# A late step of an attention block's end: moved by one or two tiles, in two parts, behind a product on GpSimd

## The chip, the cores and the metric

The kernel runs on one core of a Trainium2 chip. Its engines are TensorE (PE; its weight loads are shown as PEld), VectorE (DVE), ScalarE (ACT), GpSimd (POOL) and SyncE (SP, which here only issues DMAs). The metric is the device time of one execution in microseconds. Before the change it is 3525.12 us, the median of three runs that took 3520.41, 3525.12 and 3527.70 us. A separate profiled execution took 3519.81 us.

## The reference

A two-layer backbone over 2048 latent tokens (a grid of 32 rows by 64 columns, width 1024) with 256 context tokens. Layer 0 mixes latent attention and a gated linear attention; layer 1, which the change touches, is a two-dimensional neighbourhood attention with 16 heads of 64. What it computes, cut to this layer:

```python
# for each grid row r: kb, vb are the 8 rows of keys and values around r
s_lat = einsum('bqhd,brkhd->bhqrk', qr, kb) * scale + bias          # a table by row and column offset
s_lat = where(col_mask, s_lat, -inf)                                 # 16 columns around the query
s_ctx = einsum('bqhd,bchd->bhqc', qr, k_ctx) * scale                 # all 256 context keys
p = softmax(concatenate([s_lat, s_ctx], -1))
o = einsum('bhqk,bkhd->bqhd', p_lat, vb) + einsum('bhqc,bchd->bqhd', p_ctx, v_ctx)
# then
y = dot(o.reshape(..., 1024) * silu(z_x), w_out)
x = x + gate * y
```

Inputs and output are float32. Each query's output is a weighted sum of values, divided by the sum of its weights (the softmax's denominator), and then multiplied by the gate path's value.

## The kernel before

The whole program is written out by hand in Python and handed to a planner, which fixes the order of instructions on each engine: it simulates the engines and, whenever one is free, issues the ready instruction that was written first. `issue_after(ins)` adds an edge: what is written in its block and runs on the same engine as `ins` comes behind `ins`. Each engine then works through its own queue in the planned order.

The layer-1 attention (`odd_attention`) takes the 16 heads as 8 head pairs, j = 0 to 7; one head of a pair lies in partitions 0 to 63, the other in 64 to 127. The 2048 queries are four blocks of 512 (8 grid rows each), b0 to b3. The keys are 16 latent tiles of 128 keys (l0 to l15) and, for each block of queries, two context tiles of 128 keys. The list `units` gives a pair's 24 tiles in order: c0 twice, l0, c1 twice, l1 to l3, c2 twice, l4 to l7, c3 twice, l8 to l15.

For each tile PE makes scores (L1785, keys against the queries that can see them) into one of two PSUM tiles "st". For a latent tile, DVE adds the table of biases (L1963, "table sums", several instructions where the rectangle falls into pieces) into one of eleven SBUF tiles "opt", and ACT takes the exponential in place. For a context tile ACT takes it straight from PSUM. The products with the values come some tiles later: the list `pend` holds finished tiles, and whenever it holds five, at each second tile, `flush(2)` works off two. `tail_ctx` (L1797) makes a context tile's product with the values; the first of a block starts a new PSUM bank "o", of which there are four (L1794). `tail` (L1815) adds a latent tile's products to the banks of the blocks that it touches, and GpSimd adds the weights themselves to the running sums "oacc" (L1821), the later denominators. The first sums of a block are made from its two context tiles (L1806), on DVE for b0 and b2, on GpSimd for b1 and b3.

When the last latent tile of a block is done, `finish_blocks` ends the block. It is a generator, and each `yield` ends a step: (1) PE sums the denominators over the partitions, times -2 (L1838), into an "st" tile, ACT copies them; (2) ACT takes the logarithm (into "rl", of which there is one); (3) ACT takes the exponential of its negative, about the reciprocal; (4) a product of the two (L1849), on GpSimd for b0 and b3 of the pairs j = 0 to 6, else on DVE; (5) three DVE steps on the block's bank: a Newton step with that product (L1853), times the reciprocal (L1854), times the gate path's value "Z" (L1855); then a DMA of the result (L1856), on GpSimd's queue but for b0 of the last pair.

b0's generator is started and run to its end within one `flush` (L1915 to L1917). The others are appended to the list `ends`, and `end()`, called once a tile (L1972), takes one step of the first generator in the list, with edges behind this tile's exponential on ACT and behind the latest table sums on DVE. b1's end begins in the last tiles of its own pair, those of b2 and b3 in the next pair, after tiles l2 and l4. In the last pair b2 and b3 end together. The tiles of the gate path ("os4" and "ogate", loaded by `gates` on SP's queue, each with one buffer) are free again when L1855 has read them. In the last pair DVE and ACT also split the output weights between the tiles (L1299).

Of the kernel before, what the change touches and what calls it, by code (L numbers as in the profile page):

```python
# [88 lines left out]
class Kern:  # L89
# [1630 lines left out]
    def odd_attention(self, out, pools, left, wout):  # L1720

        nc = self.nc
        self.RT1 = self.scr("RT1", (KD, P, SEQ), F32)
        NR, NC = (len(b) for b in BLOCKS["k"])
        with ExitStack() as es:
# [62 lines left out]
            def sums(acc, bb, n=1):  # L1788

                return [acc[bb // 2][:, i].rearrange("p r c -> p (r c)")[:, (bb % 2) * 512 : (bb % 2) * 512 + n * 512] for i in range(2)]  # L1790
# [41 lines left out]
            def finish_blocks(bbs, j, O, acc):  # L1832

                n, hf, o0 = len(bbs), bbs[0] // 2, bbs[0] % 2 * 512
                den = both()
                for b, bb in enumerate(bbs):
                    for i, a in enumerate(sums(acc, bb)):
                        mm = nc.tensor.matmul(den[i * 64 : i * 64 + 64, b, :], self.mtwos[:], a, start=True, stop=True)  # L1838
                dc = exps()
                self.act(dc[:, :n], den[:, :n])  # L1840
                yield mm
                ln = self.tl(lp, [P, 2, 512], "rl", bufs=1)
                self.act(ln[:, :n], dc[:, :n], AF.Ln, scale=-1.0)
                yield
                rc = exps()
                self.act(rc[:, :n], ln[:, :n], AF.Exp, scale=-1.0)
                yield
                near = nc.gpsimd if bbs in ([0], [3]) and j < 7 else nc.vector
                near.tensor_tensor(out=ln[:, :n], in0=dc[:, :n], in1=rc[:, :n], op=ALU.mult)  # L1849
                yield  # L1850
                for b, bb in enumerate(bbs):
                    o = O.pop(bb)[:].rearrange("p r c -> p (r c)")
                    nc.vector.scalar_tensor_tensor(out=o, in0=ln[:, b], scalar=2.0, in1=o, op0=ALU.add, op1=ALU.mult)  # L1853
                    nc.vector.tensor_tensor(out=o, in0=o, in1=rc[:, b], op=ALU.mult)  # L1854
                    nc.vector.tensor_tensor(out=rc[:, b], in0=o, in1=Z[j, hf][:, o0 + b * 512 : o0 + b * 512 + 512], op=ALU.mult)  # L1855
                (nc.sync if (j, bbs) == (7, [0]) else nc.gpsimd).dma_start(self.RT1[j, :, bbs[0] * 512 : (bbs[0] + n) * 512], rc[:, :n].rearrange("p b c -> p (b c)"))  # L1856

# [45 lines left out]
            def flush(n):  # L1903

                mm = None
                for f, *a in pend[:n]:
                    mm = f(*a)
                del pend[:n]
                for x in late:
                    x[0] -= 1  # L1910
                for x in [x for x in late if x[0] <= 0]:
                    late.remove(x)
                    ends.append(finish_blocks(*x[1:]))
                    mm = next(ends[-1])
                    if x[1] == [0]:  # L1915
                        for _ in ends.pop():
                            pass  # L1917
                return mm
# [9 lines left out]
            for j in range(8):  # L1928
                OA[j] = {}, {}
                for s, (kind, n, u) in enumerate(units):  # L1930
                    g, c = divmod(n, 4)
# [183 lines left out]
            for t in range(PLAIN, NT - NCT, 2):  # L2115
# [3 lines left out]
                else:  # L2119
                    res = exps([P, 512])  # L2120
# [105 lines left out]
```

## Time and profile before

| What | Value |
|---|---|
| median of three runs | 3525.12 us (3520.41 to 3527.70) |
| the profiled execution | 3519.81 us, span from the first to the last instruction 3518.0 us |
| busy share of the span | PE 98%, DVE 68%, ACT 42%, GpSimd 30% |
| TensorE clock granted | 0.992 on average |
| layer-1 attention | about 2940 to 3370 us of the span; one head pair takes 46.5 us |

A row of a timeline gives the start in us from the span's start, the duration in us (of the whole run where a row stands for several of the same), the engine ("q" behind it is its instruction queue), the line, the operation, out<-in with the program's names, the shapes and the count; in brackets the idle time of the engine just before it, and which engine, tile and line ended it. A row of the waits reads: who waited, for whom, us in total, times, the longest. A row of stretches gives the stretch, its length, then busy us and instructions of PE, PEld, DVE, ACT and POOL, the granted clock, the share of the DMA engines and GB/s. "om,ones" marks the last of a tile's four score terms; 128x512 in L1785 is a context tile.

### The profile page before, as it was taken

Reading aid. Unit: us, or ns where it says so; the run is one execution under the profiler, and the core shown is the slowest. Engines: PE = TensorE matmul, PEld = TensorE weight load, DVE = VectorE, ACT = ScalarE, POOL = GpSimd, SP = SyncE. Lnnn points to the kernel's source line nnn. Section 1 sums busy time; section 2 is a strip of 40 time slices with the busy share of each in tenths; the row PEclk is TensorE's granted clock in tenths of the full one; section 3 lists DMA queues with packets and bytes.
Section 4 is the critical chain, followed back from the end, with each engine's and each line's share of the span. In section 5 each row is a group of like instructions: output and inputs, shape, how many; then the busy total and the mean of one; then the engine's idle time right before and its main releaser. Section 6 shows DMA issues by size and latency. Waiting matters only on the chain.

```text
span 3518.0 us, 54816 instructions
## 1 busy us (share of the span) xinstructions
PE 3431.9 (98%) x20228; PEld 2656.4 (76%) x20228; DVE 2405.5 (68%) x4509; ACT 1466.8 (42%) x2612; POOL 1061.2 (30%) x1309
## 2 busy tenths in 40 slices
PE   8999998999999999999999999999999999999899
PEld 6898987888886666665556888888888887555577
DVE  4677755888886777768877555555577884565765
ACT  4545552111113555456664345444422223555532
POOL 1343331111111334322211133333211113778711
PEclk9999999999999999999999999999999999999999
DMA  7555555232325242333634674444845546555374
GB/s 255 144 160 160 149 142 155 96 108 89 93 81 171 60 135 80 98 115 123 185 96 133 128 184 150 143 147 144 277 151 167 157 149 216 193 202 187 110 184 63
DMA packets 350111, 508.40 MB, mean 145 GB/s; under 512 B 32666, under 2 KB 233066, under 8 KB 342884
## 3 DMA queue, kind: packets, MB, share of 16 engines
q1 hardware_dynamic: 297364, 386.91, 36.3%
q0 software_dynamic: 29456, 82.14, 8.8%
q10 hardware_dynamic: 23024, 35.85, 3.0%
q8 instruction: 160, 2.62, 0.3%
q14 instruction: 107, 0.88, 0.1%
HBM read 325.99 MB, written 196.60 MB: 149 GB/s over the span
## 4 chain that ended last, share of the span: by engine, by line
PE 78%; DVE 6%; POOL 5%; DMA 5%; ACT 3%; issue 2%; SPq 1%; DVEq 0%; ACTq 0%; POOLq 0%
PE gm L133 10%; PE gm L131 10%; PE gm L132 10%; PE st L1175 10%; PE av L1085 7%; PE mx L705 4%; PE st L1785 2%; PE pu L1364 2%; PE o L1364 2%; POOL oacc L1821 2%; PE st L1364 1%; PE pj L1364 1%; PE mx L1697 1%; PE o L1815 1%; DMA adaw<-ada_w 1%
## 5 line engine op out<-in xcount | busy, mean ns | idle before, releaser
L706 DVE TENSOR_REDUCE mm<-mx 128x1 f32<-128x512 f32 (+1 forms) x656 | 389.4, 629 | 84.2 <-PE mx L705 77.2
L108 ACT ACTIVATE apt<-st 128x1024 f32<-128x1024 f32 (+1 forms) x296 | 300.2, 1015 | 303.0 <-PE st L1175 283.6
L1182 DVE TENSOR_TENSOR acc<-acc,apt 128x1024 f32<-128x1024 f32 x256 | 341.2, 1333 | 82.8 <-ACT apt L108 63.8
L1175 PE MATMUL st<-aq,akh 64*128 64x512 f32 x1728 | 312.2, 408 | 1.3 <-ACT apt L108 1.0
L1085 PE MATMUL av<-apt,av 128*64 128x512 f32 x1152 | 265.8, 598 | 0.0
L705 PE MATMUL mx<-mk,mq 96*128 96x512 f32 (+1 forms) x656 | 236.0, 373 | 5.3 <-DMA mq<-QC 4.9
L1821 POOL TENSOR_TENSOR oacc<-oacc,opt 128x528 f32<-128x528 f32 (+4 forms) x192 | 221.6, 1171 | 48.1 <-ACT opt L108 42.7
L1175 PE MATMUL st<-aq,akl 64*128 64x512 f32 (+1 forms) x1152 | 230.7, 390 | 0.0
L108 ACT ACTIVATE u<-gm 128x352 f32<-128x352 f32 (+1 forms) x140 | 68.7, 497 | 375.0 <-PE gm L133 206.1
L1175 PEld LDWEIGHTS st<-aq,akh 64*128 64x128 f32 x1728 | 152.9, 185 | 82.7 <-ACT apt L108 29.3
L1703 DVE CUSTOM_DVE_ANT_1 mx<-mx,mtab 128x105 f32<-128x105 f32 (+14 forms) x576 | 183.1, 340 | 46.9 <-PE mx L1697 35.4
L1963 DVE TENSOR_TENSOR opt<-st,tab 128x496 f32<-128x496 f32 (+16 forms) x288 | 124.3, 485 | 94.6 <-PE st L1785 93.6
L1085 PEld LDWEIGHTS av<-apt,av 128*64 128x64 f32 x1152 | 76.3, 136 | 135.2 <-issue 133.9
L108 ACT ACTIVATE opt<-opt 128x930 f32<-128x930 f32 (+9 forms) x130 | 104.7, 805 | 142.3 <-DVE opt L1963 133.3
L705 PEld LDWEIGHTS mx<-mk,mq 96*128 96x128 f32 x656 | 121.6, 189 | 17.5 <-issue 5.3
L1175 PEld LDWEIGHTS st<-aq,akl 64*128 64x128 f32 (+1 forms) x1152 | 112.3, 184 | 22.8
L220 POOL TENSOR_TENSOR oss<-oss,mhalf 128x8 f32<-128x8 f32 x68 | 112.4, 1652 | 5.4
L1552 DVE TENSOR_TENSOR onat<-gm,oss 128x512 f32<-128x512 f32 x68 | 46.9, 690 | 95.8 <-POOL oss L220 95.8
L131 PE MATMUL gm<-w1h,hhi 128*128 128x512 f32 x280 | 111.9, 400 | 0.0
L1785 PE MATMUL st<-qh,kh 64*128 64x512 f32 (+6 forms) x384 | 83.4, 429 | 27.4 <-DVE opt L1963 22.7
L133 PE MATMUL gm<-w1h,hlo 128*128 128x512 f32 x280 | 110.0, 393 | 0.0
L131 PE MATMUL gm<-w0h,hhi 128*128 128x512 f32 x272 | 109.6, 403 | 0.0
(779 smaller groups left out, 9619.5 us busy)
## 6 DMA issues: line engine op xcount, KB each, us to landing
H<-x ACTq DMA_DIRECT2D x32, 512.0 KB
adaw<-ada_w SPq DMA_DIRECT2D x64, 256.0 KB
wraw<-w_od SPq DMA_DIRECT2D x64, 256.0 KB
K1t<-okt POOLq DMA_DIRECT2D x16, 1024.0 KB, 6.6
x<-H SPq DMA_DIRECT2D x31, 512.0 KB
mtab<-rpb_q SPq DMA_DIRECT2D x16, 899.0 KB
x<-xin SPq DMA_DIRECT2D x18, 512.0 KB
x<-xin POOLq DMA_DIRECT2D x18, 512.0 KB, 5.2
```

Of the source, the lines that this page charges most:

```text
L108: return self.nc.scalar.activation(out, in_, func, **kw)
L131: self.nc.tensor.matmul(out, lh(k), rh(k), start=start and j == 0, stop=False)
L132: self.nc.tensor.matmul(out, lh(k), rl(k), start=False, stop=False)
L133: yield self.nc.tensor.matmul(out, ll(k), rh(k), start=False, stop=stop and j == n - 1)
L705: mm = nc.tensor.matmul(ps[:, :w], q[:A_QK, (t % 6) * P : (t % 6) * P + P], k[:A_QK, k0 : k0 + w], start=True, stop=True)
L706: nc.vector.tensor_reduce(out=m[:, t, n : n + 1], in_=ps[:, :w], axis=AX.X, op=ALU.max)
L1085: mm = nc.tensor.matmul(O[j, nb][i * 64 : i * 64 + 64, :w], V[j, kt // TT][:, kt % TT, i * 64 : i * 64 + 64], pts[:, i, :w], start=n == 0, ...
L1175: mm = nc.tensor.matmul(ps[:, o // 64, :w], k[o : o + r, kb, kq], Q[o : o + r, qb, :w], start=m == 0, stop=m == 4)
L1182: added = nc.vector.tensor_tensor(out=acc[:, :, :w], in0=a[:, :, :w], in1=pts[:, :, :w], op=ALU.add)
L1364: self.mm = self.nc.tensor.matmul(ps, x[:, k, :], y, start=start and k == 0 and n == 0, stop=k == self.H4 - 1 and n == 2, skip_group_check ...
L1703: nc.vector.tensor_tensor_reduce(out=s, in0=s, in1=tb[:, ri : ri + rn, ci : ci + cn], scale=1.0, scalar=-3e38, op0=ALU.add, op1=ALU.max, a ...
L1821: nc.gpsimd.tensor_tensor(out=a, in0=a, in1=pts[:, :, a0 - r0 : a1 - r0, :], op=ALU.add)
```

## The change

In `finish_blocks`, behind the product L1849: where the product ran on GpSimd, the generator yields once more, so that the steps behind it come a tile later. The three DVE steps are parted: L1853 and L1854 of all blocks of this end first, then a `yield`, then L1855 and the DMA. So L1855 and the DMA come one tile later than L1853 and L1854. Nothing else is edited; b0's generator takes the same `yield`s, but is run to its end at once.

```diff
@@ finish_blocks
                 near = nc.gpsimd if bbs in ([0], [3]) and j < 7 else nc.vector
                 near.tensor_tensor(out=ln[:, :n], in0=dc[:, :n], in1=rc[:, :n], op=ALU.mult)
                 yield
-                for b, bb in enumerate(bbs):
-                    o = O.pop(bb)[:].rearrange("p r c -> p (r c)")
+                if near is nc.gpsimd:
+                    yield
+                res = [O.pop(bb)[:].rearrange("p r c -> p (r c)") for bb in bbs]
+                for b, o in enumerate(res):
                     nc.vector.scalar_tensor_tensor(out=o, in0=ln[:, b], scalar=2.0, in1=o, op0=ALU.add, op1=ALU.mult)
                     nc.vector.tensor_tensor(out=o, in0=o, in1=rc[:, b], op=ALU.mult)
+                yield
+                for b, o in enumerate(res):
                     nc.vector.tensor_tensor(out=rc[:, b], in0=o, in1=Z[j, hf][:, o0 + b * 512 : o0 + b * 512 + 512], op=ALU.mult)
                 (nc.sync if (j, bbs) == (7, [0]) else nc.gpsimd).dma_start(self.RT1[j, :, bbs[0] * 512 : (bbs[0] + n) * 512], rc[:, :n].rearrange("p b c -> p (b c)"))
```

## The prediction

> **What bounds the kernel now.** I read the page first, then the waits of one stretch, then the timeline of its engines. j counts the eight head pairs; head pair j=2 (the stretch 3058.3 to 3104.7 us) stands for j=1 to 6, which repeat it. Tiles are l0 to l15 and the context tiles c0 to c3; b0 to b3 are the blocks of 512 queries; a block's last three DVE steps are named by line: 1853, 1854, 1855.
>
> ```profile
> PE 3431.9 (98%) x20228; PEld 2656.4 (76%) x20228; DVE 2405.5 (68%) x4509; ACT 1466.8 (42%) x2612; POOL 1061.2 (30%) x1309
> ```
>
> PE is the bound, so only idle time of PE is worth anything. Waits of that stretch (total, times, longest), and the busy time of engines in a 45 us stretch:
>
> ```profile
> POOL RT L1856 <- ACT opt L108: 10.3, 2, 5.1
> DVE opt L1963 <- PE st L1785: 7.5, 5, 2.3
> DVE o L1853 <- POOL rl L1849: 5.3, 2, 3.6
> PE st L1785 <- DVE opt L1963: 2.3, 2, 1.4
> ```
>
> ```profile
> 3085.00:3130.00 45.00, 42.57 (x394) 26.44 (x392) 26.24 (x52) 25.45 (x35) 35.10 (x31) 1.00 0.54 188
> ```
>
> DVE waits 5.3 us per pair for the GpSimd product, and PE waits 2.3 us for DVE's table sums (1963). Since PE is busy 42.57 of 45 us, those 2.3 us are nearly all that can be won: 6 x 2.3 = 13.8 us. Where they lie (PE's timeline, two answers):
>
> ```profile
> 3069.76 0.39 PE L1785 MATMUL st<-om,ones 64*128 64x480 f32 x2
> ...
> 3070.65 0.38 PE L1785 MATMUL st<-om,ones 64*128 64x480 f32 x2
> 3070.96 1.94 PE L1797 MATMUL o<-opt,ov 128*64 128x512 f32 x8
> 3072.83 0.43 PE L1785 MATMUL st<-qh,kh 64*128 64x360 f32 x2
> ...
> 3073.75 0.50 PE L1785 MATMUL st<-qh,kh 64*128 64x512 f32 x2
> ...
> 3077.96 0.32 PE L1785 MATMUL st<-om,ones 64*128 64x360 f32 x2
> ...
> 3081.53 0.49 PE L1785 MATMUL st<-qh,kh 64*128 64x480 f32 x2 [0.85 <-DVE opt L1963]
> ```
>
> ```profile
> 3083.85 1.94 PE L1797 MATMUL o<-opt,ov 128*64 128x512 f32 x8
> ...
> 3087.05 1.63 PE L1815 MATMUL o<-opt,ov 128*64 128x72 f32 x24
> 3090.11 0.43 PE L1785 MATMUL st<-qh,kh 64*128 64x352 f32 x2 [1.42 <-DVE opt L1963]
> ```
>
> The reader should see two stalls: 0.85 us before l9's scores (behind b3's steps) and 1.42 us before l13's (behind b0's).
>
> **The change, part by part.** Going through the tile loop: b0's generator is run out in one go, so for b0 nothing moves, and 7 of the 14 GpSimd products stay as they are. b1's 1855 moves from tile l0 to the next, a context tile without table sums, so DVE's order stays. b2's 1855 moves behind l5's table sums. b3 starts one step later, since b2's generator blocks the list one tile longer: its Ln, Exp and product come at l6, l7 and the first c3 tile, 1853 and 1854 behind l8's table sums, 1855 behind l9's. The instruction count is unchanged. The last pair of blocks keeps its sequence but for the two 1855. Here are the engines around b2, then around b3, then DVE around b0:
>
> ```profile
> 3069.80 0.69 DVE L1855 TENSOR_TENSOR opt<-o,ogate 128x512 f32<-128x512 f32 x1
> ...
> 3070.41 1.12 DVE L1963 TENSOR_TENSOR opt<-st,tab 128x930 f32<-128x930 f32 x1
> ...
> 3070.79 0.55 POOL L1856 DMA_DIRECT2D RT<-opt  x1
> ...
> 3071.44 1.22 DVE L1806 TENSOR_TENSOR oacc<-opt,opt 128x1024 f32<-128x1024 f32 x1
> ...
> 3072.57 1.87 DVE L1963 TENSOR_TENSOR opt<-st,tab 128x930 f32<-128x930 f32 x2
> 3072.69 2.08 POOL L1821 TENSOR_TENSOR oacc<-oacc,opt 128x682 f32<-128x682 f32 x2 [1.35 <-ACT opt L108]
> ```
>
> ```profile
> 3076.96 1.29 POOL L1849 TENSOR_TENSOR rl<-opt,opt 128x512 f32<-128x512 f32 x1
> ...
> 3078.20 2.42 POOL L1821 TENSOR_TENSOR oacc<-oacc,opt 128x506 f32<-128x506 f32 x3
> ...
> 3078.28 0.70 DVE L1853 SCALAR_TENSOR_TENSOR o<-rl,o 128x512 f32<-128x512 f32 x1 [3.55 <-POOL rl L1849]
> ...
> 3080.42 0.96 DVE L1963 TENSOR_TENSOR opt<-st,tab 128x240 f32<-128x240 f32 x2
> 3080.53 0.33 SPq L113 DMA_DIRECT2D ogate<-z  x1
> 3080.80 0.57 POOL L1856 DMA_DIRECT2D RT<-opt  x1 [0.18 <-issue]
> 3081.40 2.41 POOL L1806 TENSOR_TENSOR oacc<-opt,opt 128x1024 f32<-128x1024 f32 x1
> 3081.42 0.81 ACT L108 ACTIVATE opt<-opt 128x720 f32<-128x720 f32 x1 [2.66 <-DVE opt L1963]
> ...
> 3082.73 2.37 DVE L1963 TENSOR_TENSOR opt<-st,tab 128x930 f32<-128x930 f32 x2 [1.34 <-PE st L1785]
> ...
> 3083.47 0.63 ACT L108 ACTIVATE opt<-rl 128x512 f32<-128x512 f32 x1
> 3083.75 1.87 POOL L1821 TENSOR_TENSOR oacc<-oacc,opt 128x144 f32<-128x144 f32 x2
> ```
>
> ```profile
> 3086.89 0.69 DVE L1853 SCALAR_TENSOR_TENSOR o<-rl,o 128x512 f32<-128x512 f32 x1 [1.79 <-POOL rl L1849]
> ...
> 3089.03 1.74 DVE L1963 TENSOR_TENSOR opt<-st,tab 128x480 f32<-128x480 f32 x6
> ```
>
> *b3's stall goes: -0.85.* l8's scores end at 3077.96 + 0.32 = 3078.28, but its table sums start at 3080.42, behind b3's three steps. With the steps behind them, DVE follows the scores at once, 2.1 us sooner, and PE's 0.85 us go. DVE's 3.55 us go too, as long as the product is done by the end of l8's table sums: it ends at 3076.96 + 1.29 = 3078.25 now, a tile later perhaps at 3079.5, and these sums would end near 3078.3 + 1.2 (the delay of the next part) + 0.96 = 3080.5.
>
> *b2's output bank: +1.2 (bounds +1.1 and +2.1).* There are four "o" banks. The context products of tile c2 (1797, at 3070.96) take the bank that b2 of the pair before still holds, until its 1855 has read it: now at 3069.80 + 0.69 = 3070.49, 0.47 us before PE comes. Moved: l5's table sums start when their scores end (3069.76 + 0.39, say 3070.2), then comes the first sum (1806, written in the loop ahead of the moved step), then 1855. By the distances of starts that is 3070.2 + 1.03 + 1.13 = 3072.36, ending at 3073.05. So the context products come at 3073.1 in place of 3070.96, 2.1 us late, if PE's order stays. If the planner puts l7's scores (0.92 us, from 3072.83 to 3073.75) ahead, PE waits 0.3 us for their bank, then 0.75, and reaches the next scores at 3073.1 + 1.87 = 3074.97 in place of 3073.75: 1.2 late. I take 1.2, because no edge ties those scores to the products. Queued behind the waiting 1797 on PE are, in the order of now, l7's scores and all that follows, for which DVE's table sums and ACT's exponentials wait in turn.
>
> *b3's output bank: 0 (bounds 0 and +0.7).* The same at 3083.85: b3's 1855 now follows l9's table sums, whose two-tile group of 2.37 us makes 1.15 a tile; PE meanwhile does l10's scores, about the same time, so 0.7 us of 1855 remain, or nothing with l11's scores ahead.
>
> *PE's own arrival* at the 1.42 us stall: 3087.05 + 1.63 = 3088.68, now +1.2 - 0.85 = 3089.0 (bounds: 3088.9 and, with 2.1 and 0.7, 3090.6).
>
> *b0's stall: -0.4 (bounds 0 and all of it).* l13's scores wait for l11's table sums, these for b0's steps, these for a product on GpSimd, which is busy almost without a gap from 3072.69. There, b3's DMA (0.57 and 0.18 idle) moves behind the product, b2's DMA (0.57), now in an idle stretch of 1.35 us, comes into the busy one, and the start is 0.2 sooner with l5's table sums: -0.4 in sum. The product then ends at 3086.4, and l13's scores start at 3089.7 in place of 3090.11. Were the product issued ahead of the two adds at 3083.75 (its Exp now ends at 3084.10, just too late), 1.87 us more would go, and PE's own arrival would set the start.
>
> *Pair:* max(3089.0, 3089.7) - 3090.11 = -0.4; six pairs: **-2.4 us**.
>
> *Hidden at no cost.* b1's DMA waits in GpSimd's queue where GpSimd idles 5.1 us anyway; without that, 0.6 us. SP's next load of gates waits for b3's 1855 (3080.53) and comes 4 us later; behind it stands only the next pair's load at 3094.71:
>
> ```profile
> 3094.71 0.32 SPq L113 DMA_DIRECT2D qh<-Q  x1
> ```
>
> The result tile (one of eleven) is held one to four tiles longer; DVE's table sums wait for PE's scores alone in the waits above, so some are free; if not, a table sum would wait for the store, a few us.
>
> *Last pair (j=7): -0.6 (bounds -1.2 and +2.2).* Rows of PE, then of DVE:
>
> ```profile
> 3308.78 1.94 PE L1797 MATMUL o<-opt,ov 128*64 128x512 f32 x8 [0.47 <-DVE opt L1855]
> ...
> 3336.11 0.66 PE L1785 MATMUL st<-qh,kh 64*128 64x352 f32 x2 [4.27 <-DVE opt L1963]
> ```
>
> ```profile
> 3317.71 0.70 DVE L1853 SCALAR_TENSOR_TENSOR o<-rl,o 128x512 f32<-128x512 f32 x1 [1.18 <-POOL rl L1849]
> ```
>
> DVE splits weights here and sets the pace (PE waits 4.27 us for it), so 1.18 us of DVE idle is a gain; the bank wait, already 0.47, grows by up to 1.03 + 1.13. I take half the gain, since DVE is the later.
>
> **Sum.** -2.4 - 0.6 = -3.0 us. The profiled execution took 3519.81 us (span 3518.0, and 1.81 around it); it becomes 3516.8. It was 5.3 below the median of 3525.12, so for a median I forecast 3522.1.
>
> A rule beside the 0.47 us row: the Trainium skill (PSUM — Partial Sum Buffer, Engine vs sequencer instructions) says that matmuls start and complete in program order, so a product that waits for its bank holds all later ones. By it, the bank wait costs its full 2.1 where the planner leaves the order, which is the second rival. The row agrees, as PE stood still there.
>
> **Rivals.** *Both stalls go:* b0's product passes the two adds, and PE's arrival sets l13: 3089.0 - 3090.11 = -1.1, times six, and -1.2: -7.8, **3517.3**. For it: b0's denominator copy and Exp come on ACT behind l8's exponential, which now waits 2.66 us for l8's late table sums (3081.42) and no longer would. Against: PE's own 1.2 us from b2's bank delay the denominators too.
> *The bank wait replaces the stall:* PE's order stays, +2.1 + 0.7 - 0.85 = +1.95 on arrival. While b0's stall absorbs it, +0.5 a pair: 6 x 0.5 + 2.2 = +5.2, **3530.3**. If b0's chain comes late by as much (ACT's exponentials of the context tiles feed GpSimd's sums), 6 x 1.95 + 2.2 = +13.9, **3539.0**. It is slower by more than 0.2% from 0.8 us a pair. For it: only 0.47 us of slack; against: the planner may reorder.
> *No effect:* b3's product, ready a tile later, slips behind 2.42 us of adds and DVE waits there as before: **3525**.
>
> **Chances.** Forecast 0.36; both stalls go 0.24; no effect 0.16; bank wait absorbed 0.12, not absorbed 0.12. A median here can't tell less than about 0.2% (7 us) from nothing. Faster 0.25 (most of the first rival), same 0.60, slower 0.15. The range 3514 to 3531.5 reaches past the first rival and the absorbed bank wait.
>
> **What would show it.** DVE's wait for the product over the whole stage is now
>
> ```profile
> DVE o L1853 <- POOL rl L1849: 33.9, 14, 3.6
> ```
>
> of which b3's seven are 6 x 3.55 + 1.18 = 22.5 us; 7 waits and some 11 us should be left. PE's 0.85 us gap gone in six pairs; a new gap at 1797 behind 1855, of 0.3 to 2.1 us; the 1.42 us gap at 0.7. Wrong if 1797 shows no gap (then the banks don't matter) or the 1.42 us gap stays whole.

## The result, and the profile after

The changed kernel takes 3514.98 us (median of 11 runs, 3507.04 to 3520.56), the kernel before 3522.95 us on the same chip (11 runs, 3520.41 to 3527.7). The ratio is 0.9975 with a 95% interval of 0.9965 to 0.9984: 8.0 us faster, where 3.0 were forecast. The time lies in the predicted range, 1 us above its lower end. The profiled execution took 3510.49 us, its span is 3508.7.

The three moved steps have other line numbers now: the Newton step 1853 is 1855, the multiplication by the reciprocal 1854 is 1856, that by the gate 1855 is 1859, and the table sums 1963 are 1967. In what follows they are called Newton step, reciprocal step, gate step and table sums. First the busy times on the page of the kernel after; PE's and DVE's hardly move.

```profile
PE 3432.0 (98%) x20228; PEld 2654.7 (76%) x20228; DVE 2408.5 (69%) x4509; ACT 1466.0 (42%) x2612; POOL 1058.0 (30%) x1309
```

The waits of the whole layer-1 attention (2985 to 3361 us) in the kernel before, total, times and longest, of PE for the table sums; the row of DVE for the product stands in the prediction (33.9 us, 14 times):

```profile
PE st L1785 <- DVE opt L1963: 22.7, 19, 4.3
```

The same view of the kernel after:

```profile
PE st L1785 <- DVE opt L1967: 9.4, 15, 2.7
PE o L1797 <- DVE opt L1859: 5.7, 7, 0.8
DVE o L1855 <- POOL rl L1849: 2.9, 7, 0.9
```

DVE's wait for GpSimd's products fell from 33.9 to 2.9 us; 7 waits are left, as forecast, but the prediction had some 11 us left in them. PE's wait for table sums fell by 13.3 us; a wait of 0.81 us at the context products is new in pairs 1 to 6, and in the last pair it was 0.47 before. In the third head pair (j=2), on PE of the kernel after:

```profile
3073.37 1.94 PE L1797 MATMUL o<-opt,ov 128*64 128x512 f32 x8 [0.81 <-DVE opt L1859]
3075.24 0.51 PE L1785 MATMUL st<-qh,kh 64*128 64x512 f32 x2
...
3082.12 0.49 PE L1785 MATMUL st<-qh,kh 64*128 64x480 f32 x2
...
3084.51 0.43 PE L1785 MATMUL st<-qh,kh 64*128 64x360 f32 x2 [0.34 <-DVE opt L1967]
...
3085.35 1.94 PE L1797 MATMUL o<-opt,ov 128*64 128x512 f32 x8
...
3089.47 0.43 PE L1785 MATMUL st<-qh,kh 64*128 64x352 f32 x2
```

The reader should see the new wait for b2's bank (0.81), l9's scores without their 0.85 us gap (3082.12), and l13's scores without their 1.42 us gap (3089.47). Both pairs begin at the same place of the span, so 3089.47 against 3090.11 is the gain of the pair: 0.64 us.

To see where the 8 us come from, the attention is measured on PE's rows: its first scores, the denominators (L1838) of b1 in pairs 1 and 6, l14's scores in the last pair (the second scores with 352 columns) and the last denominators. Before:

```profile
2961.47 0.50 PE L1785 MATMUL st<-qh,kh 64*128 64x512 f32 x2 [0.69 <-ACT ovz L108]
...
3046.74 1.03 PE L1838 MATMUL st<-oacc,mtwos 128*64 128x512 f32 x4
...
3280.83 1.03 PE L1838 MATMUL st<-oacc,mtwos 128*64 128x512 f32 x4
...
3337.42 0.52 PE L1785 MATMUL st<-qh,kh 64*128 64x352 f32 x2
...
3357.33 1.94 PE L1838 MATMUL st<-oacc,mtwos 128*64 128x512 f32 x8
```

After:

```profile
2962.39 0.50 PE L1785 MATMUL st<-qh,kh 64*128 64x512 f32 x2 [0.69 <-ACT ovz L108]
...
3046.71 1.03 PE L1838 MATMUL st<-oacc,mtwos 128*64 128x512 f32 x4
...
3276.06 1.03 PE L1838 MATMUL st<-oacc,mtwos 128*64 128x512 f32 x4
...
3330.29 0.43 PE L1785 MATMUL st<-qh,kh 64*128 64x352 f32 x2 [1.08 <-DVE opt L1967]
...
3348.14 1.94 PE L1838 MATMUL st<-oacc,mtwos 128*64 128x512 f32 x8
```

That gives three stretches. The *head* (first scores to b1 of pair 1, with the first crossing from one pair to the next): 85.27 us before, 84.32 after. The five *middle* pairs: 234.09 before, 229.35 after. The *last* stretch (b1 of pair 6 to the end): 76.50 before, 72.08 after. In the trace of before one middle pair is 1.3 us longer than the others, because PE was slowed there for some 4 us (3184.9 to 3189; the granted clock over 3185 to 3190 is 0.66); so a middle pair is given below by the median of the five: 46.53 before, 45.81 after. In sum: head -0.95, middle 5 x -0.72 = -3.6, last -4.4, together -9.0 us against -8.0 between the medians. More than half of what the forecast missed was made in the last stretch.

The last stretch can be parted at l14's scores of the last pair. They come at 56.59 us of the stretch before and at 54.23 after, 2.36 us sooner. From there on PE waits for nobody in either trace, and still it takes 19.91 us before and 17.85 after, because before the first matmuls of this tail run at about half speed (2.97 against 1.61 us for the values' products, shown further below). So of the 4.42 us, 2.36 are an earlier arrival and 2.06 are PE's speed.

### The profile page after: what moved, and what is told of

Same layout as the page of the kernel before. It is cut to its first block, busy times and chain, and to the rows that moved or that the text cites. A ratio compares the mean times of both kernels' runs of the same rounds, so it can differ in the third digit from the quotient of the medians.

```text
span 3508.7 us, 54807 instructions
## 1 busy us (share of the span) xinstructions
PE 3432.0 (98%) x20228; PEld 2654.7 (76%) x20228; DVE 2408.5 (69%) x4509; ACT 1466.0 (42%) x2612; POOL 1058.0 (30%) x1309
## 4 chain that ended last, share of the span: by engine, by line
PE 84%; DVE 5%; DMA 4%; issue 2%; POOL 2%; ACT 2%; SPq 0%; DVEq 0%; ACTq 0%; POOLq 0%
PE st L1175 10%; PE gm L131 10%; PE gm L133 10%; PE gm L132 10%; PE av L1085 7%; PE mx L705 4%; PE st L1785 3%; PE o L1364 2%; PE pu L1364 2%; PE o L1815 2%; PE st L1364 1%; PE o L1797 1%; PE pj L1364 1%; PE mx L1697 1%; PE up L124 1%
## 5 line engine op out<-in xcount | busy, mean ns | idle before, releaser
L706 DVE TENSOR_REDUCE mm<-mx 128x1 f32<-128x512 f32 (+1 forms) x656 | 389.3, 630 | 82.9 <-PE mx L705 75.9
L1821 POOL TENSOR_TENSOR oacc<-oacc,opt 128x528 f32<-128x528 f32 (+6 forms) x192 | 220.5, 1168 | 41.7 <-ACT opt L108 36.0
L108 ACT ACTIVATE opt<-opt 128x930 f32<-128x930 f32 (+7 forms) x130 | 104.5, 805 | 132.3 <-DVE opt L1967 126.6
L132 PE MATMUL gm<-w1l,hhi 128*128 128x512 f32 x280 | 109.6, 391 | 0.0
```

What stands on the lines that cost most here:

```text
L108: return self.nc.scalar.activation(out, in_, func, **kw)
L132: self.nc.tensor.matmul(out, lh(k), rl(k), start=False, stop=False)
L706: nc.vector.tensor_reduce(out=m[:, t, n : n + 1], in_=ps[:, :w], axis=AX.X, op=ALU.max)
L1821: nc.gpsimd.tensor_tensor(out=a, in0=a, in1=pts[:, :, a0 - r0 : a1 - r0, :], op=ALU.add)
```

## The experiments

Two theories were put to the test first. **Q**: what counts is the order of DVE's queue, that is, which table sums stand ahead of a step that waits for GpSimd. **W**: it is enough that the steps are written later, so that they don't meet the product. The two traces differ in DVE's queue in one more place than the prediction foresaw. Nothing in the edit touches b0, but the planner now lets l11's table sums overtake b0's reciprocal and gate steps. DVE's timeline of the kernel after:

```profile
3086.40 0.70 DVE L1855 SCALAR_TENSOR_TENSOR o<-rl,o 128x512 f32<-128x512 f32 x1 [0.32 <-POOL rl L1849]
3087.01 0.94 DVE L1967 TENSOR_TENSOR opt<-st,tab 128x480 f32<-128x480 f32 x2
3087.86 0.69 DVE L1856 TENSOR_TENSOR o<-o,opt 128x512 f32<-128x512 f32 x1
```

All runs at one glance. Ratio and interval are to the kernel before on the same chip; head, middle pair (median) and last stretch are of the profiled execution, in us.

| Run | Median, us | Ratio (95% interval) | Head | Pair | Last |
|---|---|---|---|---|---|
| before | 3521.3 to 3523.1 | 1 | 85.3 | 46.53 | 76.5 |
| the change | 3514.98 | 0.9975 (0.9965 to 0.9984) | 84.3 | 45.81 | 72.1 |
| extra yield alone | 3522.54 | 0.9998 (0.9990 to 1.0007) | 85.3 | 46.80 | 75.9 |
| split alone | 3515.65 | 0.9979 (0.9969 to 0.9988) | 85.1 | 46.34 | 73.4 |
| b3 late, b2 whole | 3513.56 | 0.9972 (0.9961 to 0.9983) | 84.2 | 46.10 | 70.8 |
| l11 kept behind b0 | 3515.29 | 0.9980 (0.9971 to 0.9988) | 84.5 | 45.83 | 73.9 |
| before, b0 behind l11 | 3509.39 | 0.9965 (0.9951 to 0.9979) | 83.3 | 45.45 | 73.7 |
| pairs 6 and 7 alone | 3519.68 | 0.9989 (0.9980 to 0.9998) | 85.3 | 46.58 | 72.4 |
| first sum behind gate step | 3516.03 | 0.9979 (0.9971 to 0.9988) | 84.6 | 46.16 | 72.4 |
| before, 12 matmuls in the gap | 3524.18 | 1.0009 (1.0001 to 1.0018) | 85.3 | 46.50 | 79.7 |
| before, 4 matmuls in the gap | 3519.17 | 0.9994 (0.9985 to 1.0003) | 85.3 | 46.48 | 74.6 |
| all steps behind | 3510.53 | 0.9972 (0.9960 to 0.9985) | 83.3 | 45.25 | 75.4 |
| before, no running sums | 3510.89 | 0.9970 (0.9958 to 0.9981) | 85.2 | 46.55 | 64.7 |
| two forms joined | 3508.70 | 0.9959 (0.9946 to 0.9973) | 83.3 | 45.21 | 72.8 |

The stretches are those of one trace each. Before and "extra yield alone" have the same order on DVE, and differ by 0.3 us in the pair and 0.6 in the last stretch; a difference of that size in one trace shows nothing by itself.

### The two halves of the change

The extra yield alone (the kernel before with this):

```diff
                 yield
+                if near is nc.gpsimd:
+                    yield
                 for b, bb in enumerate(bbs):
```

> Only the extra step behind a GpSimd product; the three last DVE steps stay together. b3's last steps then come at the second c3 tile, which has no table sums, so DVE's queue is the same as before. Theory Q (what counts is DVE's queue: where l8's and l11's table sums stand against b3's and b0's last steps): no change against before, 3523 us, PE's gaps of 0.85 and 1.42 us both still there in each pair. Theory W (what counts is that the steps come later in the program, so that DVE does not meet the GpSimd product): most of the 8 us, about 3517 us.

Measured: no change, 0.9998. In its trace DVE does the same instructions in the same order as before. W falls: a step written a tile later that keeps its place in DVE's queue is no later.

The split alone (the change without those two lines):

```diff
                     nc.vector.tensor_tensor(out=o, in0=o, in1=rc[:, b], op=ALU.mult)
+                yield
+                for b, o in enumerate(res):
                     nc.vector.tensor_tensor(out=rc[:, b], in0=o, in1=Z[j, hf]...
```

> Only the parting of L1853, L1854 from L1855 by a tile; no extra step behind a GpSimd product. In DVE's queue b2's L1855 stands behind l5's table sums and the first sum, as in the change, but b3's L1853 and L1854 still stand ahead of l8's table sums, and l11's behind all of b0's steps. Theory Q: the price of b2's output bank without the gain: PE's new gap of 0.8 us at the c2 context products, the rest of it 0.4 us at l7's scores; slower than before by 0 to 1.2 us a pair, 3523 to 3530 us. Theory W (later steps, less waiting): faster than before, about 3519 us.

Measured: 0.9979, almost the whole gain, and against the expectation of Q (slower) as well as of W (half the gain). In its pair j=2, PE and then DVE:

```profile
3074.96 1.94 PE L1797 MATMUL o<-opt,ov 128*64 128x512 f32 x8 [0.81 <-DVE opt L1857]
...
3091.77 0.43 PE L1785 MATMUL st<-qh,kh 64*128 64x352 f32 x2 [1.16 <-DVE opt L1965]
```

```profile
3088.55 0.70 DVE L1853 SCALAR_TENSOR_TENSOR o<-rl,o 128x512 f32<-128x512 f32 x1 [1.50 <-POOL rl L1849]
```

Its pairs come out just past the lower end of Q's 0 to 1.2 us slower: the gap of 0.85 is gone, the one of 0.81 is new, l13's is at 1.16, and a pair is 0.2 us shorter. The gain is in the last stretch, -3.1 us, where neither theory had looked. This run turned the question from "which gap of a pair" to "what happens in the last pair".

### b3 late and b2 whole, and l11's table sums kept in their place

The change, but b3 two tiles later and parted, b2 and b1 whole:

```diff
                 if near is nc.gpsimd:
                     yield
+                    yield
...
-                yield
+                if near is nc.gpsimd:
+                    yield
```

> The change for b3 alone: b1's and b2's three steps stay together, and b3 gets two extra steps, so that its last steps land where the change puts them. DVE's queue is that of the changed kernel but for b2's L1855, ahead of l5's table sums as before. Theory Q with the output bank priced by the changed kernel's trace (0.81 us gap at the c2 context products and about 0.4 at l7's scores): 0.8 to 1.2 us a pair less than the changed kernel, 6 to 8 us over seven pairs, 3507 to 3509 us. If the bank wait only takes the place of another wait: as the changed kernel, 3515 us.

Measured: 0.9972, no better than the change within the intervals, as the second expectation had it. Pair j=2 on PE:

```profile
3074.48 1.94 PE L1797 MATMUL o<-opt,ov 128*64 128x512 f32 x8
...
3093.45 0.43 PE L1785 MATMUL st<-qh,kh 64*128 64x352 f32 x2 [1.04 <-DVE opt L1969]
```

The wait for the bank is gone, and PE stands 1.04 us at l14's scores instead: a pair is 0.3 us longer than with the change (46.1 in all five middle pairs, where the change has 45.8 in four). A price taken away at one place came back at the next.

The change, with an edge that keeps l11's table sums behind b0's last step:

```diff
+ with self.tc.issue_after(self.b0_done.ins) if n == 11 else ExitStack():
      bias = nc.vector.tensor_tensor(...)      # the table sums
```

> The changed kernel with an order edge that puts l11's table sums behind all of b0's steps in DVE's queue, as they stood before the change; the rest of DVE's queue as in the changed kernel. Theory Q: in pairs 1 to 6 the chain product, three steps, table sums ends at about the time that PE comes (3089.6 against 3089.5 us in the changed kernel's second pair), so 0 to 0.2 us a pair, but in the last pair, where weight splits stand between b0's steps, PE's gap before l13's scores comes back at 3 to 4 us: 3518 to 3520 us in all. Theory W: as the changed kernel, 3515 us.

Measured: 0.998, the same as the change. That is the number of W, which had already fallen; Q's number is missed. DVE and then PE of pair j=2:

```profile
3085.37 0.70 DVE L1855 SCALAR_TENSOR_TENSOR o<-rl,o 128x512 f32<-128x512 f32 x1 [0.32 <-POOL rl L1849]
...
3087.52 1.74 DVE L1969 TENSOR_TENSOR opt<-st,tab 128x480 f32<-128x480 f32 x6
```

```profile
3088.60 0.43 PE L1785 MATMUL st<-qh,kh 64*128 64x352 f32 x2
```

In this execution the pair begins 0.8 us earlier in the span (3045.92 in place of 3046.74), so b0's Newton step starts at 39.45 us of the pair where it started at 3086.89 - 3046.74 = 40.15 before: 0.7 us sooner. l13's scores follow without a gap at 42.68, before at 43.37: also 0.7. So in the middle pairs the earlier product is enough, and the overtaking of l11's table sums, which Q had made the cause, adds nothing there. In the last stretch Q's expectation holds: PE stands still for 3.96 us before l13's scores, where the change has 0.52, and the stretch is 1.8 us longer (73.9 against 72.1). The medians don't show it.

### Only the last pair

The whole change, but for blocks of pairs 6 and 7 alone:

```diff
-                if near is nc.gpsimd:
+                if near is nc.gpsimd and j > 5:
                     yield
...
-                yield
+                if j > 5:
+                    yield
```

> The whole change, but only in the blocks of head pairs 6 and 7, so only the last crossing from one pair to the next and the last pair have it; pairs 0 to 5 are those of the kernel before. Theory L (most of the gain is made in the last pair, where DVE sets the pace): the stretch of the last pair is 6 to 7 us shorter, as with the whole change, and the time is 3523.1 - 6.6 = 3516.5 (3515.5 to 3517.5). Theory S (the gain is the sum of equal small gains in every pair, as the prediction had it): two of eight crossings, some -2: 3521.

Head and middle are those of before, and the last stretch is 72.4 us, 4.1 shorter: theory L holds for the place of the gain, though its 6 to 7 us were too much. The ratio stands for -3.9 us, its interval for -7.0 to -0.7. Theory S's -2 lies in that as well, so it is the stretches of the trace that decide.

### What slows the last pair: GpSimd beside DVE's splits

The kernel before, without GpSimd's running sums in the last pair:

```diff
-                    nc.gpsimd.tensor_tensor(out=a, in0=a, in1=pts[...], op=ALU.add)
+                    if j < 7:
+                        nc.gpsimd.tensor_tensor(out=a, in0=a, in1=pts[...], op=ALU.add)
```

> The kernel before, with work left out: in the last pair GpSimd adds no latent tile's weights to the running sums, and a block's first sum is its first context tile plus 1 (one input in place of two), so the last pair's denominators are not the reference's. It asks why DVE's 16 splits of the output weights take 0.69 to 3.04 us each in the last pair (23.9 us in sum). Theory K (they are slowed by GpSimd's work at the same time): all 16 come down to about 0.69 us, 11 us in sum, DVE has 12 us less to do, PE's 4.27 us gap before l13's scores goes or falls under 1.5 us, and the time is 8 to 13 us shorter: 3508 to 3513. Theory O (the splits are slow from something else: ACT's copy, the loads, the place of the weights): they stay above 1.2 us in the mean, and what is gained is the first sums alone, under 3 us: 3518.5 to 3521.

Measured: 0.997, and a last stretch of 64.7 us, 11.8 shorter. The timeline of DVE and GpSimd in the kernel before:

```profile
3321.48 3.04 DVE L1299 TENSOR_TENSOR ov<-opt,ov 128x512 fp32r<-128x512 f32 x1
3321.58 2.38 POOL L1806 TENSOR_TENSOR oacc<-opt,opt 128x1024 f32<-128x1024 f32 x1
...
3323.92 2.35 POOL L1821 TENSOR_TENSOR oacc<-oacc,opt 128x144 f32<-128x144 f32 x2
3324.44 2.37 DVE L1299 TENSOR_TENSOR tab<-opt,tab 128x512 fp32r<-128x512 f32 x1
```

And without the running sums:

```profile
3319.18 0.67 DVE L1299 TENSOR_TENSOR ov<-opt,ov 128x512 fp32r<-128x512 f32 x1
...
3320.64 0.69 DVE L1299 TENSOR_TENSOR tab<-opt,tab 128x512 fp32r<-128x512 f32 x1 [0.79 <-ACT tab L108]
```

The same split takes 3.04 us beside GpSimd's sums and 0.67 us without them. All 16 splits took 23.9 us before and take 13.4 here; 13 of the 16 are at 0.67 to 0.69. Theory K holds. In all fourteen traces, each split of 128x512 in this stretch that met no computing GpSimd instruction took 0.67 to 0.69 us. The 11.8 us are not the price of the splits alone: they became 10.5 us shorter, the first sums had one input fewer, and PE, whose granted clock over the stretch was 0.93 before and is 1.00 here, takes 17.8 us from l14's scores on in place of 19.9. How the 11.8 are shared isn't separated. The long splits of before end 0.56 and 0.54 us behind the end of the GpSimd work beside them (3324.52 against 3323.96, 3326.81 against 3326.27), as if they did their work once that work was done. The Trainium skill (SBUF — State Buffer, Who interferes with whom) calls the port pair that DVE and GpSimd share an exclusive lock, and says that a DVE instruction with two SBUF inputs contends with a GpSimd instruction that reads SBUF. These rows agree.

With the change the 16 splits take 22.3 us, 1.6 less, and DVE's wait of 1.18 us for b3's product is gone.

### PE at half clock after standing still

The prediction's rows show PE standing still for 4.27 us before l13's scores of the last pair. Further rows of the kernel before, where the second shows values' products (1.61 us for the same shape at full speed, below):

```profile
3321.71 0.77 PE L1785 MATMUL st<-qh,kh 64*128 64x480 f32 x2 [1.78 <-DVE opt L1963]
...
3338.76 2.97 PE L1815 MATMUL o<-opt,ov 128*64 128x93 f32 x24
```

Twelve, then four, matmuls with a tile of zeros (made ahead) as weights fill that gap (they add nothing to the bank that they write):

```diff
+ if j == 7 and n == 13:
+     o = OA[7][0][3][:].rearrange("p r c -> p (r c)")
+     for _ in range(12):                                  # 4 in the second run
+         nc.tensor.matmul(o[:64], zero[:], M[1][:, :512].bitcast(F32), start=False, stop=False, skip_group_check=True)
  mm = scores(...)
```

> The kernel before, with 12 matmuls of zero weights (128x512, some 0.25 us each, 3 us in sum) added to a live output bank just ahead of l13's scores of the last pair, where PE stands still for 4.27 us and then runs its next matmuls at twice their time (the 352-column scores 0.66 us in place of 0.43) from 3336.1 to 3342.7. They add nothing to the result. Theory P (the slow stretch follows from PE's standing still, and costs the time it takes): the slow matmuls are gone and the end comes about 3 us sooner, 3520. Theory D (DVE's table sums and splits set the end of the last pair, and PE's slow matmuls are hidden or have another cause): 3523, no change.

> The kernel before with 4 in place of 12 zero matmuls in front of l13's scores of the last pair. With 12 of them they took 10.46 us (0.87 us each), so l13's scores started some 6 us late, but then ran at 0.43 us in place of 0.66 and the last denominator was only 3.2 us late. Four take 3.5 us, which fits into the 4.27 us in which PE stands still. Theory P (the slow stretch follows from PE's standing still and its time is lost): l13's scores start where they did, run at 0.43 us, and the last pair is 2.7 to 3.3 us shorter: 3521.3 - 3 = 3518.3. Theory D (the slow matmuls are hidden behind DVE or GpSimd): 3521.3, no change.

PE with twelve:

```profile
3330.85 10.46 PE L1964 MATMUL o<-om,zero 128*64 128x512 f32 x24
3341.25 0.43 PE L1785 MATMUL st<-qh,kh 64*128 64x352 f32 x2
```

PE with four:

```profile
3332.86 3.59 PE L1964 MATMUL o<-om,zero 128*64 128x512 f32 x8
3337.01 0.43 PE L1785 MATMUL st<-qh,kh 64*128 64x352 f32 x2 [0.55 <-DVE opt L1969]
...
3338.66 1.61 PE L1815 MATMUL o<-opt,ov 128*64 128x93 f32 x24
```

The twelve were mis-sized: I had taken 0.25 us each from a row that counts two records to a matmul, and they took 0.87, so l13's scores came some 6 us late. They still ran at once at 0.43 us, and the stretch was only 3.2 us longer. With four, which fit into the gap, scores take 0.43 in place of 0.66 us and the values' products 1.61 in place of 2.97. The half clock follows from PE's standing still. What it costs in time is 1.9 us of the stretch in these two traces (74.6 against 76.5), under the 2.7 to 3.3 that theory P expected: PE now waits 0.55 and, at the next denominators, 0.75 us for DVE. At the medians no difference is shown (0.9985 to 1.0003).

The other traces bear the cost out where nothing hides it, in the tail from l14's scores to the last denominators. In the six whose granted clock stays at full there it takes 17.7 to 17.9 us; in the seven where a slowed spell falls into it, 18.8 to 20.0. (The run with four matmuls, with its wait of 0.75 us, takes 18.8.)

The Trainium skill (TensorE: Matmul & The Clock Gate, What's actually happening) gives one idle window of about 3.4 us as what halves the clock. The 4.27 us gap agrees. The row at 3321.71 doesn't: the 480-column scores ran there at 0.77 in place of 0.49 us behind a gap of 1.78, so a PE that is only partly idle is slowed too.

### The two gaps of a pair, taken apart

The kernel before, with only b0's reciprocal and gate steps moved behind l11's table sums (the generator stops ahead of them, and its rest is run in an `issue_after` of those sums):

```diff
                     nc.vector.scalar_tensor_tensor(out=o, in0=ln[:, b], ...)
+                    if bbs == [0]:
+                        yield True
...
+                    if kind == "l" and n == 11:
+                        with self.tc.issue_after(bias.ins):
+                            for _ in self.b0:
+                                pass
```

> The kernel before, with one thing moved: b0's multiplication by the reciprocal and by the gate are issued behind l11's table sums, in all eight pairs. b2 and b3 stay as they were. It asks what holds l13's scores (the 1.42 us gap of each pair): DVE's order at b0, or the chain of GpSimd that ends in b0's product. Theory Q (DVE's order): l11's table sums come 2 x 0.69 = 1.4 us sooner, so PE reaches l13 without a gap, at its own arrival of 3088.7 in place of 3090.1: -1.4 a pair, 6 x 1.4 = -8.4, about 3514.7 beside 3523.1. Theory G (the product's end sets the rest of the chain too, and the lost time comes back at the next wait behind it): at most -0.4 a pair, 3520.5 to 3523.

Measured: 0.9965. PE in pair j=2:

```profile
3082.11 0.49 PE L1785 MATMUL st<-qh,kh 64*128 64x480 f32 x2 [0.82 <-DVE opt L1966]
...
3089.18 0.43 PE L1785 MATMUL st<-qh,kh 64*128 64x352 f32 x2
...
3090.58 0.43 PE L1785 MATMUL st<-qh,kh 64*128 64x352 f32 x2 [0.47 <-DVE opt L1966]
```

l13's gap of 1.42 us is gone, l9's stays, and 0.47 us appear at l14's scores, since b0's steps now stand ahead of l12's table sums: 46.53 - 45.45 = 1.08 us a pair, not 1.4. Q holds but for that. The median fell by 11.9 us, more than Q's 8.4, because the head (-2.0) and the last stretch (-2.8) gained too. This one move, without anything of the change, does about as much as the change: the intervals overlap, and a pair takes 45.45 against 45.81.

The change, with b2's first sum written behind the gate step instead of ahead of it (for the unit with l5):

```diff
-                    if s in FIRST_SUMS:
+                    if s in FIRST_SUMS and s != 11:
                         ... sum_ctx(...)
...
                     end()
+                    if s == 11:
+                        ... sum_ctx(...)
```

> The changed kernel, with b2's first sum (1.13 us on DVE) written behind the moved multiplication by the gate instead of ahead of it, so that the output bank of b2 of the pair before is read out 1.1 us sooner. It asks whether the 0.81 us gap that PE has in each pair at the context products, which the change brought in, is a price of the whole pair. Theory B (it is): the gap goes, -0.8 in each of seven pairs, 3515 - 5.6 = 3509.4. Theory C (the chain through GpSimd to b0's steps sets the pair's end, so PE loses the same time at l11's or l13's scores instead): the 0.81 gap goes and a gap behind DVE's table sums grows by as much, 3514 to 3516.

Measured: 0.9979, no better than the change. PE and then DVE:

```profile
3093.01 0.43 PE L1785 MATMUL st<-qh,kh 64*128 64x352 f32 x2 [1.01 <-DVE opt L1967]
```

```profile
3089.18 0.69 DVE L1855 SCALAR_TENSOR_TENSOR o<-rl,o 128x512 f32<-128x512 f32 x1 [1.50 <-POOL rl L1849]
3089.79 0.94 DVE L1967 TENSOR_TENSOR opt<-st,tab 128x480 f32<-128x480 f32 x2
3090.64 0.69 DVE L1856 TENSOR_TENSOR o<-o,opt 128x512 f32<-128x512 f32 x1
```

The 0.81 us wait for the bank is gone, and 1.01 us come at l14's scores (the next expectation calls them l13's; they are the second of the two with 352 columns). PE was earlier, but the product on GpSimd was not: DVE waits 1.50 us for it at the Newton step, with the table sums of l11 and l12 queued behind. So the new wait was no price of the pair; it had only moved a loss forward. Theory C holds for that order.

The same, with all three of b0's steps behind l11's table sums:

```diff
                     yield
+                if bbs == [0]:
+                    yield True
                 res = [O.pop(bb)...]
...
+                    if kind == "l" and n == 11:
+                        with self.tc.issue_after(bias.ins):
+                            for _ in self.b0:
+                                pass
```

> The changed kernel with two more moves: b2's first sum behind its gate step (as in the run that took the 0.81 us gap away and got a gap of 1.01 us before l13's scores for it), and all three of b0's steps, the Newton step that waits for GpSimd's product included, behind l11's table sums. It asks whether that second gap was DVE standing still for the product (1.50 us) with l11's table sums queued behind it. Theory Q (DVE's queue order): both gaps go, a pair takes 45.0 us in place of 45.8, six pairs -4.8, and the time is about 3509 to 3510 beside 3515 for the change alone. Theory C (the chain through GpSimd sets a pair's length whatever DVE's order): 3514 to 3516.

PE and DVE:

```profile
3089.45 0.43 PE L1785 MATMUL st<-qh,kh 64*128 64x352 f32 x2 [0.38 <-DVE opt L1970]
```

```profile
3086.27 0.70 DVE L1857 SCALAR_TENSOR_TENSOR o<-rl,o 128x512 f32<-128x512 f32 x1 [0.67 <-POOL rl L1849]
```

A pair takes 45.25 us (45.0 expected), so Q holds: with l11's table sums ahead of the waiting step, the gap shrinks from 1.01 to 0.38. By the intervals, the median of 3510.53 is not shown to be below that of the run before it; the last stretch is 3.3 us longer than with the change: there one split takes 4.11 us and PE stands still for 4.49.

### Two forms joined

The form above in pairs 0 to 6, the order of "b3 late, b2 whole" from the last crossing on:

```diff
+                    if (j, bbs) == (6, [3]):
+                        yield
-                if bbs == [0]:
+                if bbs == [0] and j < 7:
                     yield True
...
-                yield
+                if (j < 6 or near is nc.gpsimd or (j, bbs) == (6, [1])) and bbs != [0]:
+                    yield
```

> Two forms joined: pairs 1 to 6 as in the run with all of b0's steps behind l11's table sums and b2's first sum behind its gate step (45.24 us a pair in its trace, 75.4 us from the last-but-one pair's b1 denominators to the last denominator), and the last crossing and the last pair in the order of the run with only b3 later and b2 whole (70.8 us for that stretch). Theory A (the two parts are independent, the splits' durations go with DVE's order): the stretch is 70.5 to 71.5 us and the trace is 4 to 5 us shorter than with the first form throughout: a ratio of 0.996 to the kernel before, about 3507 to 3508.5 beside 3522. Theory M (which splits fall beside which sums on GpSimd depends on the microsecond, not only on the order): the splits' sum differs from 20.8 us by more than 1.5 us and the stretch is 72 us or more: 3509 to 3512.

Measured: 0.9959 (0.9946 to 0.9973), 3508.70 us, the lowest median of all; its interval still overlaps that of the change. The last stretch took 72.8 us, not the 70.8 of the run whose order it has. PE of "b3 late, b2 whole", then of this run:

```profile
3333.05 0.43 PE L1785 MATMUL st<-qh,kh 64*128 64x352 f32 x2 [0.44 <-DVE opt L1969]
...
3333.91 1.61 PE L1815 MATMUL o<-opt,ov 128*64 128x93 f32 x24
```

```profile
3328.40 0.66 PE L1785 MATMUL st<-qh,kh 64*128 64x352 f32 x2 [1.08 <-DVE opt L1973]
...
3329.87 2.48 PE L1815 MATMUL o<-opt,ov 128*64 128x93 f32 x24
```

In the two traces PE, DVE and ACT run the same instructions in the same order from b1's denominators of pair 6 on. The splits took 22.0 in place of 20.8 us, not the 1.5 more of theory M, and l14's scores come only 0.5 us later in the stretch. The other 1.5 us lie behind them, where PE waits for nobody: here a slowed spell falls on that tail, while in the other run it fell earlier (3323.3 to 3330.2), ahead of a wait for DVE. So theory A falls, and M names one of two causes: the order of the queues alone doesn't fix this stretch, because the meetings of splits and sums, and the place of the slowed spell, differ from trace to trace.

## Why the prediction was right in sign and short in size

- **b3's stall goes, -0.85: right.** l9's scores come without a gap.
- **b2's output bank, +1.2 with l7's scores ahead: right in mechanism, somewhat small.** The forecast put the context products at 3073.1 behind a wait of 0.75 us; they came at 3073.37 behind 0.81. The next scores came at 3075.24 in place of 3073.75, 1.5 us late, within the bounds of 1.1 and 2.1.
- **b3's output bank, 0: right.** 3085.35 shows no wait; l11's scores went ahead and waited 0.34 us for table sums, which the sum didn't have.
- **PE's own arrival at l13, 3089.0: too early.** It was 3089.47, from the two points above for the most part.
- **b0's stall, -0.4: near in size, wrong in what sets the start.** In the changed kernel b0's Newton step comes 0.46 us sooner in the pair (3086.40 - 3046.71 = 39.69 against 40.15), by a chain like the one forecast. But "for b0 nothing moves" was wrong: l11's table sums no longer stand behind all three of b0's steps, and PE's own arrival sets l13's scores: 3089.47 - 3090.11 = -0.64, where the forecast had the chain set them with -0.4. With l11 kept in place the chain itself gave 0.7. That the pair, -0.72 by the median of the middle pairs, is off by only 0.3 is partly luck, since the late arrival took back a part of what the overtaking gave. Head and middle together gave -0.95 - 3.6 = -4.5 us against -2.4.
- **Last pair, -0.6 (bounds -1.2 and +2.2): the step that failed.** It gave -4.4, outside its bounds. The prediction saw that DVE sets the pace there and priced DVE's idle time (1.18 us), but took the durations of the splits and PE's speed as given. Both move with the order. Shown by runs: without GpSimd's running sums beside them the splits take 10.5 us less and the stretch 11.8, and without PE's half clock behind the 4.27 us gap it takes 1.9 less. The 4.4 us part into 2.06 behind l14's scores, where PE's speed alone differs, and 2.36 ahead of them. How far the wait of 1.18 us, and the 1.6 us by which the splits became shorter, make up those 2.36 was only argued, not shown.
- **The rivals.** "Both stalls go" (3517.3, -7.8) named the right end for the pairs, both gaps gone and PE's arrival setting l13, but by another way: the product did not pass the adds. "The bank wait replaces the stall" didn't come, because the planner put l7's scores ahead. "No effect" didn't come: DVE no longer waits for b3's product. Of the three outcomes, "faster" (0.25) came about, by 8.0 us where the prediction took 7 as the least that a median can tell.

## What to carry to other kernels

When a step waits for a slow engine, ask what is queued behind it on its own engine; here moving two steps of b0 behind one table sum, in the kernel before, gained about as much as the whole change. Taking away a visible gap gained nothing while the chain behind the next gap stayed as it was: the run without the 0.81 us wait lost the time again at l14's scores. In a stretch where another engine sets the pace, take the spread of an instruction's durations (0.69 to 3.04 us for one split) as a sign that part of its price depends on what runs beside it, and widen the bounds by that. Widen them too by a slowed spell of the clock, which cost 1.5 us more in one of two traces with the same order.

## What the hardware showed that I had not expected

- PE ran at half speed behind gaps much shorter than 4 us: 0.77 in place of 0.49 us behind a gap of 1.78, and for some 4 us in the middle of the attention in the trace of before, behind a 1.43 us gap. Of the five other runs that keep this gap in every pair, two show such a spell and three don't.
- One DVE subtraction of 128x512 with both inputs in SBUF took from 0.67 to 4.11 us, by what GpSimd did beside it.
- A 128x512 float32 matmul with 64 output partitions took 0.87 to 0.90 us when all went to the same 64 partitions (3.59 us for four, 10.46 for twelve). The denominators' matmuls, of the same shape and alternating between the two halves, take 1.03 us for four records, 0.26 each, against 0.44 for a record here. Why was not tried.
